# Reciprocal root in 9 instead of 12 VectorE operations; the sample tokens' convolution as one product and one sum, two heads at a time

## Chip, cores and metric

The program runs on 1 core of one Trainium2 chip. The metric is the device time of one execution in microseconds (us). Engines: TensorE (PE; its weight loads PEld overlap the matmuls), VectorE (DVE), ScalarE (ACT), GpSimd (POOL), and SyncE (SP), which issues most DMAs. Tiles live in SBUF or, behind matmuls, in PSUM banks.

## What is computed

One inference step of a two-layer trunk: 512 prompt tokens and 8 sample tokens with 1024 features. Layer 0 mixes by a gated DeltaNet (gdn), layer 1 by dilated sliding-window attention (dsw); behind each mixer stands a squared-ReLU MLP. The change touches gdn's convolution and single-token step for the sample tokens, and every 1/sqrt. The reference, cut:

```python
def l2norm(x):
    return xf * lax.rsqrt(jnp.sum(xf * xf, axis=-1, keepdims=True) + EPS)

def causal_conv_silu(x, buf, w):              # GDN_CONV = 4 taps
    xe = jnp.concatenate([buf.astype(x.dtype), x], axis=1)
    y = sum(xe[:, j:j + T] * w[j] for j in range(GDN_CONV))
    return jax.nn.silu(y), xe[:, T:]

def gdn_mixer(x, conv_buf, s0, w_in, conv_w, a_log, dt_bias, o_norm, w_out):
    ...
    qkv, new_buf = causal_conv_silu(qkv, conv_buf, conv_w)
    ...
    q = jnp.repeat(l2norm(q), rep, axis=2) * (GDN_DK ** -0.5)
    k = jnp.repeat(l2norm(k), rep, axis=2)
    beta = jax.nn.sigmoid(b.astype(f32))
    g = -jnp.exp(a_log.astype(f32)) * jax.nn.softplus(a.astype(f32) + dt_bias.astype(f32))
    o, s_new = gated_delta_chunked(q, k, v, g, beta, s0.astype(f32))
    o = rmsnorm(o, o_norm) * jax.nn.silu(z)
    y = o.reshape(B, T, GDN_V_DIM).astype(x.dtype) @ w_out
```

The recurrence is S_t = e^g S_(t-1) + beta k (v - e^g S_(t-1)^T k)^T and o_t = S_t^T q. There are 8 query/key heads, and 16 value heads of 128 x 128 states.

## The kernel before

**Stages.** Four stages follow each other on the one core: load and gdn to about 800 us, the first mlp to 1200, dsw to 1775, the second mlp to the end. The moving operand of every projection is the residual stream, features on partitions, split into a high and a low part. A projection (`proj`, L165 to L167) makes three matmuls for each of eight blocks of 128 features and each half (260 columns) of the tokens, into one of two PSUM banks called mm; then ACT or DVE empties the bank. 24 matmuls fill one bank, or 12 in the output projection of one pair, emptied by DVE in L892.

**Order.** The program text gives the dependencies. A scheduler with a simulated timeline writes the instructions of each engine in one fixed order, which the engine then works through. Six methods carry `@urgent`, a priority of 2000: decay, invert, merge, scan, sample, out. What is left fills in around them.

**gdn.** Eight pairs of value heads p = 0..7 come one after the other, each pair's first half ahead of the pair before it. For pair p:

- key: project k, sums of squares, reciprocal root "nk" (L558), and from it the columns `col` (L561 to L563).
- decay: one DMA on SP's queue reads the cumulated log-decay rows Dg into ET (L595), DVE subtracts (L596), ACT takes exponentials (L597, L598), DVE makes E (L603). ET has two buffers; one comes free after the scan of the pair before.
- invert: E's diagonal blocks go through DRAM (L629, L632), POOL solves them in 31 steps (L638, L641), and two DMAs (L642, L646) bring the result back as held<-D.
- query: project q, the sample's q and k (`sample_qk`), reciprocal root "nq" (L574).
- merge: DVE transposes (L653 to L655) behind held<-D, then PE products px (L660).
- scan: PE and DVE in turn over four chunks: pk L709, R L712, pv L715, pS L720, S L724, po L731 and L735, osb L739.
- sample: convolution of v (`sample_conv`), for each of the two heads 8 matmuls sks against its state (L816) and four DVE operations (L817 to L820), then the transpose sut of u on PE (L826), a trip through DRAM, and the state's update on POOL (L835, L838).
- out: reciprocal root "ro", DVE scales osb (L862), PE transposes otr (L867), DVE and ACT make the operand onh/onl of the output projection (L869 and the split). The last pair does it for its chunks in several cuts.

**What the change touches.** `rsqrt` (L211 to L223) makes an estimate from the bits of x in two operations (L216, L217), a factor (L218), and three rounds of three operations (L220 to L222), all on DVE. It is called 44 times: 27 times before dsw, 17 times in it. `sample_conv` (L762 to L772) is called three times for each pair: q, k, and the two v tiles together; each call makes eight DVE operations and one tanh on ACT. The history of three taps (`hist`) and the new value (`news`) lie in two parts of the stage's tile `held`.

The profile calls all small tiles base, since they are parts of one tile.

## Time and profile before

| | us |
|---|---|
| median of 3 runs | 2164.85 |
| lowest, highest run | 2163.49, 2175.41 |
| profiled execution, span from the first to the last instruction (its only time on the page) | 2168.5 |
| PE busy | 1989.6 |
| PEld busy | 1950.9 |
| DVE busy | 1349.5 |
| ACT busy | 899.4 |
| POOL busy | 535.6 |

Mean granted TensorE clock over the span: 0.950. PE is busy 92% of the span, so the time is read from where PE is not busy, and from what ended each of these idle stretches. In the rows below, a group's row has the line, engine, operation, output<-input with partitions x elements, the count, the total, the mean in ns, and the idle time before; a row of the timeline has the start and the length in us and, in brackets, the idle time before it and what ended it; a row of the waits has total, number and longest.

### The profile page before, as it was taken

Reading aid. Unit: us, or ns where it says so; the run is one execution under the profiler, and the core shown is the slowest. Engines: PE = TensorE matmul, PEld = TensorE weight load, DVE = VectorE, ACT = ScalarE, POOL = GpSimd, SP = SyncE. Lnnn points to the kernel's source line nnn. Section 1 sums busy time; section 2 is a strip of 40 time slices with the busy share of each in tenths; the row PEclk is TensorE's granted clock in tenths of the full one; section 3 lists DMA queues with packets and bytes.
Section 4 is the critical chain, followed back from the end, with each engine's and each line's share of the span. In section 5 each row is a group of like instructions: output and inputs, shape, how many; then the busy total and the mean of one; then the engine's idle time right before and its main releaser. Section 6 shows DMA issues by size and latency. Waiting matters only on the chain. (4 is left out here: it accounts for less than half of the span.)

```text
span 2168.5 us, 41683 instructions
## 1 busy us (share of the span) xinstructions
PE 1989.6 (92%) x16361; PEld 1950.9 (90%) x16361; DVE 1349.5 (62%) x3332; ACT 899.4 (41%) x2416; POOL 535.6 (25%) x821
## 2 busy tenths in 40 slices
PE   7677889896969789999999999999999989999999
PEld 6677778896969679999999999999999989999998
DVE  6754856785766584544556467676766785544544
ACT  5434444444334353223244555555555444233231
POOL 4253264355253230000002133232332250000000
PEclk8889989988979889999999999999999999999999
DMA  5334554764655538666676675534445343333332
GB/s 145 68 71 114 149 157 127 223 181 128 204 150 158 168 96 303 228 238 242 232 248 227 221 242 141 140 108 123 120 128 137 97 115 88 89 98 89 94 92 79
DMA packets 416277, 328.54 MB, mean 152 GB/s; under 512 B 48408, under 2 KB 404568, under 8 KB 413896
## 3 DMA queue, kind: packets, MB, share of 16 engines
q1 hardware_dynamic: 416080, 325.88, 50.4%
q8 instruction: 128, 2.10, 0.4%
q14 instruction: 69, 0.57, 0.1%
HBM read 302.19 MB, written 132.83 MB: 201 GB/s over the span
## 5 line engine op out<-in xcount | busy, mean ns | idle before, releaser
L165 PE MATMUL mm<-split,whi 128*128 128x260 f32 (+1 forms) x2960 | 866.7, 293 | 3.8 <-ACT split L178 2.5
L167 PE MATMUL mm<-split,wlo 128*128 128x260 f32 (+1 forms) x2960 | 851.8, 288 | 9.4 <-DVE wlo L132 9.4
L166 PE MATMUL mm<-split,whi 128*128 128x260 f32 (+1 forms) x2960 | 851.8, 288 | 8.7 <-DVE split L179 8.6
L166 PEld LDWEIGHTS mm<-split,whi 128*128 128x128 f32 (+1 forms) x2960 | 567.1, 192 | 12.3 <-DVE split L179 10.5
L167 PEld LDWEIGHTS mm<-split,wlo 128*128 128x128 f32 (+1 forms) x2960 | 566.5, 191 | 11.8 <-DVE wlo L132 10.9
L165 PEld LDWEIGHTS mm<-split,whi 128*128 128x128 f32 (+1 forms) x2960 | 567.6, 192 | 7.2 <-ACT split L178 3.7
L132 DVE TENSOR_TENSOR wlo<-raw,whi 128x1024 fp32r<-128x1024 f32 (+1 forms) x273 | 341.0, 1249 | 195.3 <-ACT whi L131 177.7
L131 ACT CAST whi<-raw 128x1024 fp32r<-128x1024 f32 (+1 forms) x273 | 285.8, 1047 | 411.7 <-PE mm L166 396.1
L167 PE MATMUL mm<-hh,wlo 128*128 128x260 f32 x1024 | 288.8, 282 | 0.0
L166 PE MATMUL mm<-hl,whi 128*128 128x260 f32 x1024 | 288.8, 282 | 0.0
L165 PE MATMUL mm<-hh,whi 128*128 128x260 f32 x1024 | 288.1, 283 | 0.0
L167 PEld LDWEIGHTS mm<-hh,wlo 128*128 128x128 f32 x1024 | 193.0, 188 | 0.0
L166 PEld LDWEIGHTS mm<-hl,whi 128*128 128x128 f32 x1024 | 192.8, 188 | 0.0
L165 PEld LDWEIGHTS mm<-hh,whi 128*128 128x128 f32 x1024 | 192.3, 188 | 0.0
L335 DVE TENSOR_TENSOR t<-mm,bc 128x260 f32<-128x260 f32 x128 | 54.8, 428 | 153.0 <-PE mm L167 153.0
L191 POOL TENSOR_TENSOR acc<-acc,sq 128x260 f32<-128x260 f32 x42 | 37.8, 909 | 382.0 <-ACT sq L190 381.3
L638 POOL TENSOR_TENSOR fs<-Ft,held 128x60 f32<-128x60 f32 (+24 forms) x248 | 100.5, 405 | 89.2 <-DMA Ft<-D 58.7
L131 ACT CAST hh<-q 128x260 fp32r<-128x260 f32 x128 | 52.5, 410 | 122.1 <-DVE q L322 122.1
L165 PE MATMUL mm<-onh,whi 128*128 128x260 f32 x256 | 90.3, 356 | 13.0 <-DVE base L892 7.9
L530 DVE SCALAR_TENSOR_TENSOR conv<-pre,held,conv 128x512 f32<-128x512 f32 x96 | 77.6, 808 | 30.1 <-POOL pre L508 27.2
L641 POOL TENSOR_TENSOR held<-held,fs 128x60 f32<-128x60 f32 (+24 forms) x248 | 90.5, 365 | 18.5
L132 DVE TENSOR_TENSOR hl<-q,hh 128x260 fp32r<-128x260 f32 x128 | 54.9, 429 | 57.0 <-ACT hh L131 57.0
(374 smaller groups left out, 3319.4 us busy)
## 6 DMA issues: line engine op xcount, KB each, us to landing
out_dram<-in_cache_kv_w_dram SPq DMA_DIRECT2D x112, 832.0 KB
raw<-in_dsw_w_in_dram SPq DMA_DIRECT2D x72, 512.0 KB
raw<-in_mlp_w_up_dram SPq DMA_DIRECT2D x64, 512.0 KB
raw<-in_mlp_w_down_dram SPq DMA_DIRECT2D x64, 512.0 KB
raw<-in_gdn_w_in_dram SPq DMA_DIRECT2D x48, 512.0 KB
S<-in_state_gdn_dram SPq DMA_DIRECT2D x16, 512.0 KB
raw<-in_gdn_w_out_dram SPq DMA_DIRECT2D x16, 512.0 KB
ub<-Du SPq DMA_DIRECT2D x16, 512.0 KB
```

What stands on the lines that cost most here:

```text
L131: nc.scalar.copy(hi, src)
L132: nc.vector.tensor_tensor(lo, src, hi.bitcast(F32), ALU.subtract)
L165: nc.tensor.matmul(ps[:m], lhsT=w[0][:, k, :m], rhs=xh[:, s], start=k == 0, stop=False)
L166: nc.tensor.matmul(ps[:m], lhsT=w[0][:, k, :m], rhs=xl[:, s], start=False, stop=False)
L167: nc.tensor.matmul(ps[:m], lhsT=w[1][:, k, :m], rhs=xh[:, s], start=False, stop=k == nk - 1)
L191: nc.gpsimd.tensor_tensor(acc[:, s], acc[:, s], t, ALU.add)
L335: nc.vector.tensor_tensor(t, ps, r2[:, s], ALU.mult)
L530: nc.vector.scalar_tensor_tensor(a, pre[:, j : j + NP], convw[:, ft, j : j + 1], a, ALU.mult, ALU.add)
L638: nc.gpsimd.tensor_tensor(tmp[:, :m, :n], Ft[:, None, j + 1 :, j].to_broadcast([P, m, n]), Uo[:, :m, j : j + 1].to_broadcast([P, m, n]), A ...
L641: nc.gpsimd.tensor_tensor(Uo[:, :m, j + 1 :], Uo[:, :m, j + 1 :], tmp[:, :m, :n], ALU.add)
```

## The change

Three edits, and all comments and docstrings go:

1. `rsqrt` makes the estimate in one operation on the bits, then one step with a polynomial in x y^2, then one Newton step: 9 operations.
2. `hist` and `news` become one part with four taps side by side. `sample_conv` takes two feature tiles at a time (q with k, and both v): one product over 128 x 64, one sum over the taps, tanh, one operation. Three calls of eight DVE operations become two of three; a pair has one tanh less.
3. `sample` makes the matmuls sks of both heads into one bank, and the four DVE operations once for both.

DVE has 308 instructions less in all: 132 in the reciprocal roots, 144 in the convolution, 32 in the sample; 257 of them stand before 800 us. ACT has 8 less; PE, POOL and SP have as many as before.

```diff
     def rsqrt(self, pool, x, eng, tag):
         n = x.shape[1]
-        y, t, z = (self.tile(pool, [P, n], F32, tag=f"{tag}{i}", name=f"{tag}{i}", bufs=2) for i in range(3))
-        yi = y.bitcast(I32)
-        self.nc.vector.tensor_scalar(yi, x.bitcast(I32), 1, None, ALU.logical_shift_right)
-        eng.tensor_scalar(yi, yi, -1.0, float(0x5F3759DF), ALU.mult, ALU.add)
-        eng.tensor_scalar(z, x, -0.5, None, ALU.mult)
-        for _ in range(3):
-            eng.tensor_tensor(t, y, y, ALU.mult)
-            eng.tensor_tensor(t, t, z, ALU.mult)
-            eng.scalar_tensor_tensor(y, t, 1.5, y, ALU.add, ALU.mult)
+        y, t, u = (self.tile(pool, [P, n], F32, tag=f"{tag}{i}", name=f"{tag}{i}", bufs=2) for i in range(3))
+        eng.tensor_scalar(y.bitcast(I32), x.bitcast(I32), -0.5, float(0x5F300000), ALU.mult, ALU.add)
+        eng.tensor_tensor(t, y, y, ALU.mult)
+        eng.tensor_tensor(t, t, x, ALU.mult)
+        eng.tensor_scalar(u, t, 0.44643426, -1.3888901, ALU.mult, ALU.add)
+        eng.tensor_tensor(u, u, t, ALU.mult)
+        eng.scalar_tensor_tensor(y, u, 1.94250179, y, ALU.add, ALU.mult)
+        eng.scalar_tensor_tensor(t, y, -0.5, y, ALU.mult, ALU.mult)
+        eng.tensor_tensor(t, t, x, ALU.mult)
+        eng.scalar_tensor_tensor(y, t, 1.5, y, ALU.add, ALU.mult)
         return y
...
-        Ufs, T64, hist, news = [part("Uf0", P), part("Uf1", P)], part("T64", 64)[:64], part("hist", 3 * NS), part("news", NS)
+        Ufs, T64, hist = [part("Uf0", P), part("Uf1", P)], part("T64", 64)[:64], part("hist", 4 * NS).rearrange("p f (b j) -> p f b j", j=CONV)
+        news = hist[:, :, :, 3]
...
-            nc.scalar.copy(hist[:, i :: 8, :], ps[:, :96].rearrange("p (s j) -> p s j", s=4))
+            nc.scalar.copy(hist[:, i::8, :, :3], ps[:, :96].rearrange("p (s b j) -> p s b j", s=4, j=3))
...
-            def sample_conv(self, i0, n, f0):
-                a, b_ = self.a, K.tile(gp, [P, 2, NS], F32, tag="sb", name="sb", bufs=12)[:, :n]
-                fs, d = slice(f0, f0 + n), slice(i0, i0 + n)
-                wj = lambda j: convw[:, fs, j : j + 1].to_broadcast([P, n, NS])
-                nc.vector.tensor_tensor(a[:, d], news[:, fs], wj(3), ALU.mult)
-                for j in range(3):
-                    nc.vector.tensor_tensor(b_, hist[:, fs, j::3], wj(j), ALU.mult)
-                    nc.vector.tensor_tensor(a[:, d], a[:, d], b_, ALU.add)
-                nc.scalar.activation(b_, a[:, d], AF.Tanh)
-                nc.vector.scalar_tensor_tensor(a[:, d], b_, 1.0, a[:, d], ALU.add, ALU.mult)
+            def sample_conv(self, i0, fs):
+                a = self.a[:, i0 : i0 + 2]
+                taps = K.tile(gp, [P, 2, NS, CONV], F32, tag="sp", name="sp", bufs=4)
+                b_ = K.tile(gp, [P, 2, NS], F32, tag="sb", name="sb", bufs=4)
+                nc.vector.tensor_tensor(taps, hist[:, fs], convw[:, fs, None, :].to_broadcast([P, 2, NS, CONV]), ALU.mult)
+                nc.vector.tensor_reduce(a, taps, axis=AX.X, op=ALU.add)
+                nc.scalar.activation(b_, a, AF.Tanh)
+                nc.vector.scalar_tensor_tensor(a, b_, 1.0, a, ALU.add, ALU.mult)
...
-                self.sample_conv(0, 1, self.fts[0])
-                self.sample_conv(1, 1, self.fts[1])
+                self.sample_conv(0, slice(self.p, self.p + 9, 8))
...
-                self.sample_conv(2, 2, self.fts[2])
+                self.sample_conv(2, slice(self.fts[2], self.fts[2] + 2))
...
+                be, eg = (sbc[:, i, 2 * p : 2 * p + 2] for i in range(2))
+                ps = K.bank("sks")
+                pst = ps[:, :32].rearrange("p (v b t) -> p v b t", v=2, t=2)
                 for v in range(2):
-                    h = 2 * p + v
-                    be, eg = sbc[:, 0, h], sbc[:, 1, h]
-                    ps = K.bank("sks")
-                    pst = ps[:, :16].rearrange("p (b t) -> p b t", t=2)
-                    S0 = self.S0s[v]
                     for b in range(NS):
-                        nc.tensor.matmul(pst[:, b], lhsT=S0[:, b], rhs=kqs[:, b], start=True, stop=True)
-                    nc.vector.tensor_tensor(u_[:, v], pst[:, :, 0], eg, ALU.mult)
-                    nc.vector.tensor_tensor(u_[:, v], a[:, 2 + v], u_[:, v], ALU.subtract)
-                    nc.vector.tensor_tensor(u_[:, v], u_[:, v], be, ALU.mult)
-                    nc.vector.tensor_tensor(o_[:, v], pst[:, :, 1], eg, ALU.mult)
+                        nc.tensor.matmul(pst[:, v, b], lhsT=self.S0s[v][:, b], rhs=kqs[:, b], start=True, stop=True)
+                nc.vector.tensor_tensor(u_, pst[:, :, :, 0], eg, ALU.mult)
+                nc.vector.tensor_tensor(u_, a[:, 2:4], u_, ALU.subtract)
+                nc.vector.tensor_tensor(u_, u_, be, ALU.mult)
+                nc.vector.tensor_tensor(o_, pst[:, :, :, 1], eg, ALU.mult)
```

With other instructions the scheduler writes another order on every engine. Three places follow, in the words of the instruction streams. Lines of the changed kernel are its own: a line L596 of before is L599 there, L520 is L523, L534 is L537, L739 is L742, L816 is L814, L817 to L820 are L815 to L818, L826 is L824, L892 is L890.

DVE in pair 2, behind the last osb of its scan (L739), before. The four operations of each head's chain are L817, L820, L818 and L819; L596 waits for the ET of the next pair:

```order
L739 TENSOR_TENSOR osb<-osb,po 128x256
L817 TENSOR_TENSOR base<-sks,held 128x8
L820 TENSOR_TENSOR base<-sks,held 128x8
L818 TENSOR_TENSOR base<-base 128x8
L819 TENSOR_TENSOR base<-base,held 128x8
L596 TENSOR_TENSOR ET<-ET,held 128x1024
L892 TENSOR_TENSOR base<-base,mm 128x260
L859 SCALAR_TENSOR_TENSOR base<-base 128x8
L892 TENSOR_TENSOR base<-base,mm 128x260
L132 TENSOR_TENSOR wlo<-raw,whi 128x1024
L817 TENSOR_TENSOR base<-sks,held 128x8
L820 TENSOR_TENSOR base<-sks,held 128x8
```

The same place on DVE in the changed kernel:

```order
L742 TENSOR_TENSOR osb<-osb,po 128x256
L599 TENSOR_TENSOR ET<-ET,held 128x1024
L857 SCALAR_TENSOR_TENSOR base<-base 128x8
L815 TENSOR_TENSOR base<-sks,held 128x16
L818 TENSOR_TENSOR base<-sks,held 128x16
L816 TENSOR_TENSOR base<-base 128x16
L817 TENSOR_TENSOR base<-base,held 128x16
L890 TENSOR_TENSOR base<-base,mm 128x260
L820 TENSOR_TENSOR base<-base 128x16
```

One chain for both heads now stands behind ET's subtraction, where one head's chain stood ahead of it and the other's behind it. The joint chain stands behind L599 in pairs 1, 2, 3 and 5 too, ahead of it in pairs 0 and 4, and in pair 6 behind the transposes of merge.

PE in pair 2 from the end of the scan to sut, the changed kernel (S_2541 and S_2543 are the two heads' states, mm<-onh or onl the output projection, mm<-split the next projection; the run of twelve mm is three rows four times over, shown once):

```order
L738 MATMUL po<-S,kq 128x256
L814 MATMUL sks<-base,S_2541 128x2 x8
L814 MATMUL sks<-base,S_2543 128x2 x8
L165 MATMUL mm<-onh,whi 128x260
L166 MATMUL mm<-onl,whi 128x260
L167 MATMUL mm<-onh,wlo 128x260
...
L824 MATMUL sut<-base 16x128
L165 MATMUL mm<-split,whi 128x260
```

Before, the same twelve mm stood between the two heads' sks, and 35 mm of the next projection between the second sks and sut: 47 matmuls beside the sks, where 12 stand now. In the other pairs it is 57 before and 20 now (pair 0), 44 and 22, 24 and 12 (pair 3), 30 and 28, 44 and 30, 24 and 12 (pair 6).

DVE at the first two waits for ET, about 77 to 93 us of the profile, before (L520 scales the first projections, L521 the sample's part of them, and L534 makes the first value tile's input, conv, complete somewhat later):

```order
L222 SCALAR_TENSOR_TENSOR base<-base 128x4
L596 TENSOR_TENSOR ET<-ET,held 128x1024
L534 SCALAR_TENSOR_TENSOR conv<-tanh,conv 128x512
L561 TENSOR_TENSOR base<-held,base 128x8
L596 TENSOR_TENSOR ET<-ET,held 128x1024
L520 TENSOR_TENSOR pre<-pre,bc 128x512
L521 TENSOR_TENSOR held<-held,bc 128x8
```

The same place in the changed kernel:

```order
L537 SCALAR_TENSOR_TENSOR conv<-tanh,conv 128x512
L523 TENSOR_TENSOR pre<-pre,bc 128x512
L576 TENSOR_SCALAR base<-base 128x20
L524 TENSOR_TENSOR held<-held,bc 128x8
L599 TENSOR_TENSOR ET<-ET,held 128x1024
L851 TENSOR_SCALAR base<-base 128x4
L216 TENSOR_SCALAR base<-base 128x16
L770 TENSOR_TENSOR base<-held 128x64
L533 SCALAR_TENSOR_TENSOR conv<-pre,held,conv 128x512
L599 TENSOR_TENSOR ET<-ET,held 128x1024
```

L520's successor now stands ahead of both waits for ET instead of behind them.

More of the change, by code (lines that the diff above doesn't have):

```diff
@@ L374, in gdn @@
         gp = setup.enter_context(tc.tile_pool(name="gset", bufs=1))
-        sizes = dict(Uf0=U * P, Uf1=U * P, T64=U * 64, hist=32 * 3 * NS, news=32 * NS, eyeU=8 * 32, convw=32 * CONV, tri=P, Uo0=8 * 32, Uo1=8 * 32, tail=32 * 3, beg=160, gcl=128, egc=192, sbc=256, id8=8, onorm=1, alog=16, dtb=16, bat=160)
+        sizes = dict(Uf0=U * P, Uf1=U * P, T64=U * 64, hist=32 * 4 * NS, eyeU=8 * 32, convw=32 * CONV, tri=P, Uo0=8 * 32, Uo1=8 * 32, tail=32 * 3, beg=160, gcl=128, egc=192, sbc=256, id8=8, onorm=1, alog=16, dtb=16, bat=160)
         held = cp.tile([P, sum(sizes.values())], F32, name="held")
```

## The prediction

> **What bounds the kernel now.** I read first the span, then the engines' busy times by stage (windows of the trace), then the waits of TensorE and VectorE in the one stage where TensorE waits.
>
> ```profile
> span 2168.5 us, 41683 instructions
> ...
> core 0: us, PE busy (x) PEld busy (x) DVE busy (x) ACT busy (x) POOL busy (x), PEclk, DMA share, GB/s
> 0.00:800.00 800.00, 649.12 (x5217) 620.88 (x5218) 540.22 (x1536) 333.50 (x966) 325.21 (x657) 0.87 0.52 145
> ...
> 1200.00:1775.00 575.00, 553.92 (x4599) 545.86 (x4598) 401.10 (x1057) 296.21 (x945) 177.03 (x120) 1.00 0.51 144
> ```
>
> The windows shown are load with gdn, and dsw; the two mlp stages, left out, hold no edit. TensorE (PE) is idle for 800 - 649.1 = 150.9 us in the first and 575 - 553.9 = 21 us in the second, so what an edit on VectorE (DVE) can win lies nearly all in the first 800 us. There the granted clock (PEclk) averages 0.87, in dsw 1.00: 0.13 x 800 = 104 us of full-speed time are lost beside the idle time.
>
> ```profile
> PE sut L826 <- DVE base L819: 34.5, 5, 13.2
> PE px L660 <- DMA held<-D: 21.4, 3, 11.3
> PE pk L709 <- DVE S L724: 8.7, 5, 4.2
> PE mm L166 <- DVE split L179: 8.1, 4, 5.4
> PE mm L165 <- DVE base L892: 7.9, 3, 6.4
> PE sut L826 <- DVE base L767: 2.7, 1, 2.7
> DVE ET L596 <- DMA ET<-Dg: 40.3, 8, 8.2
> DVE held L653 <- DMA held<-D: 37.7, 5, 9.9
> ```
>
> These are waits in 0 to 800 us: total, times, longest. PE's largest are for DVE, at the lines that the change touches (sut, the transpose of the sample's u). But DVE itself sits idle 40.3 + 37.7 = 78 us on DMAs, in L596 (E and ET of the next pair) and L653 (merge). An engine that works its list in order and stands before a DMA is not made faster by fewer instructions ahead of that place.
>
> **What leaves DVE.**
>
> ```profile
> L221 DVE TENSOR_TENSOR base<-base 128x24 f32<-128x24 f32 (+7 forms) x132 | 28.8, 219 | 2.3
> L222 DVE SCALAR_TENSOR_TENSOR base<-base 128x24 f32<-128x24 f32 (+7 forms) x132 | 27.1, 206 | 2.7
> L220 DVE TENSOR_TENSOR base<-base 128x24 f32<-128x24 f32 (+7 forms) x132 | 24.9, 190 | 2.4
> L770 DVE TENSOR_TENSOR base<-base 128x8 f32<-128x8 f32 (+1 forms) x72 | 18.0, 251 | 0.3
> L769 DVE TENSOR_TENSOR base<-held 128x8 f32<-128x8 f32 (+1 forms) x72 | 14.9, 216 | 3.5 <-ACT held L419 3.1
> L767 DVE TENSOR_TENSOR base<-held 128x8 f32<-128x8 f32 (+1 forms) x24 | 6.8, 285 | 0.0
> L772 DVE SCALAR_TENSOR_TENSOR base<-base 128x8 f32<-128x8 f32 (+1 forms) x24 | 4.5, 187 | 0.5 <-ACT base L771 0.5
> L474 DVE TENSOR_TENSOR held<-held 128x64 f32<-128x64 f32 x1 | 0.2, 224 | 0.0
> L1255 DVE TENSOR_REDUCE base<-mxt 1x8 f32<-1x128 f32 x8 | 2.2, 272 | 0.0
> ```
>
> Each line: total us, then mean ns of one. Reciprocal root: 396 of its instructions take 80.8 us, 204 ns each; 44 calls go from 12 to 9, so 132 x 0.204 = 26.9 us less. Convolution: 192 instructions of 44.2 us become 48. The two new forms don't occur in the trace. The product over 128x64 is bounded by L474, 0.224, and the slower L767, 0.285; the sum over taps by nothing below L772's 0.187 and L1255's 0.272, which runs through 128 elements of a partition where the new one runs through 64. I take 0.224 (the same size) and 0.272: 16 x (0.224 + 0.272 + 0.187) = 10.9, so 33.3 less; the other ends move it by 1.4 us. The sample's u: 64 instructions become 32, about 6 less at L772's price. Together 66 us by full durations. But independent small instructions follow each other faster than they last:
>
> ```profile
> 251.11 0.16 DVE L772 SCALAR_TENSOR_TENSOR base<-base 128x8 f32<-128x8 f32 x1
> 251.19 0.16 DVE L216 TENSOR_SCALAR base<-base 128x4 int32<-128x4 int32 x1
> ...
> 255.41 0.30 DVE L222 SCALAR_TENSOR_TENSOR base<-base 128x4 f32<-128x4 f32 x2
> ```
>
> L772 lasts 0.16 us, and L216 starts 0.08 after it. At that price the 308 instructions that go are worth 25 us. So DVE has 25 to 66 us less to do, 257/308 of it before 800 us: 21 to 55 of 540, 4 to 10%. What of this reaches the end is counted place by place.
>
> **Term A, the first values' transposes.**
>
> ```profile
> 83.00 0.69 DVE L520 TENSOR_TENSOR pre<-pre,bc 128x512 f32<-128x512 f32 x1
> ...
> 93.06 0.69 DVE L534 SCALAR_TENSOR_TENSOR conv<-tanh,conv 128x512 f32<-128x512 f32 x1
> 93.90 1.09 PE L694 MATMUL vtr<-base,conv 128*128 128x128 f32 x4 [11.76 <-DVE base L221]
> ```
>
> The transposes read conv, so what released them is L534's end at 93.75, not the L221 that the row names. DVE needs 10.06 us from L520 to that L534, for 35 instructions. In the new order L520's successor stands ahead of both waits for ET, some 20 instructions stand between the second wait and this end, and PE has 38 instead of 20 matmuls between the two groups of transposes. About 15 instructions less at that pace, with L520's 0.69 among them, is 2.7 us; 18 matmuls at a spacing of 0.12 (below) are 2.2 us of cover. I take **-5**; ends: 0, if the wait for ET moves as much later, and -11.8, the whole wait.
>
> **Term B, the tail.**
>
> ```profile
> 778.87 1.60 DVE L221 TENSOR_TENSOR base<-base 128x4 f32<-128x4 f32 x1
> 780.53 2.34 POOL L838 TENSOR_TENSOR S<-S,ub 128x1024 f32<-128x1024 f32 x1
> 780.60 2.29 DVE L222 SCALAR_TENSOR_TENSOR base<-base 128x4 f32<-128x4 f32 x1
> 783.81 1.11 PE L867 MATMUL otr<-base,osb 128*128 128x128 f32 x4 [7.48 <-DVE osb L862]
> ```
>
> In the last pair PE waits 7.48 us on a reciprocal root whose L222 takes 2.29 us beside POOL's L838, though it has 128x4 elements and 0.21 as its mean; the L221 before it takes 1.60 instead of 0.22. With three instructions fewer ahead, the last may be done before L838 starts. I take **-3**, L222's 2.1 and most of three instructions at 0.37 (term D); ends: 0 (the stall falls on L862 instead) and -4.6, L221's 1.4 as well.
>
> By the Trainium skill, GPSIMD Engine Reference, section "Specifications", GpSimd's SBUF interface is shared with VectorE, with contention for VectorE instructions that have two SBUF inputs. L222 reads two tiles, so the trace agrees; but L862, the next that PE waits for, does too, and by this rule the stall would merely go over to it, for -0.7 instead of -3.
>
> **Term C, the sample's chain.** The rows are those of pair 2.
>
> ```profile
> 355.43 0.37 SPq L595 DMA_DIRECT2D ET<-Dg  x1
> 364.04 1.37 DVE L596 TENSOR_TENSOR ET<-ET,held 128x1024 f32<-128x1024 f32 x1 [5.79 <-DMA ET<-Dg]
> 364.62 0.28 PE L165 MATMUL mm<-split,whi 128*128 128x260 f32 x1
> 364.74 0.28 PE L166 MATMUL mm<-split,whi 128*128 128x260 f32 x1
> 367.90 0.38 PE L826 MATMUL sut<-base 128*16 128x128 f32 x1 [2.88 <-DVE base L819]
> 368.51 0.42 PE L166 MATMUL mm<-split,whi 128*128 128x260 f32 x1
> 368.73 0.42 PE L167 MATMUL mm<-split,wlo 128*128 128x260 f32 x1
> ```
>
> The first head's chain ran ahead of L596, the second's behind it and behind L132. In the new order there is one chain for both, directly behind the wait for ET. It ends some 1.4 us sooner, as L132 (1.21) now follows it, but sut stands behind 12 matmuls of projections instead of 47: 35 x 0.12 = 4.2 us that covered the wait now come after it. Net +2.7; I take +2.5 here and in pair 1, which the order changes alike (44 to 22). In pair 4 the chain now stands ahead of the wait for ET, so sut needn't wait; but the projections behind it need DVE to empty their two banks, so I give it -2. In pair 0, whose sut wait is the 2.7 row, the chain is ahead too: -2.7. Pairs 3, 5 and 6 have no clear sign. Sum **0**; ends: -11.3 (pair 4's whole wait, the second longest) and +15 (2.5 in each of six pairs).
>
> **Term D, merge.** px waits for DMAs that end a chain which begins with the key's reciprocal root: 12 instructions from 251.19 to 255.41, 4.4 us, 0.37 each among others. Three fewer are 1.1 us, in three waits **-3**; ends: 0 and twice that.
>
> **Term E, the other DVE waits** (pk 8.7, L166 8.1, L165 7.9; 24.7 together) shrink with DVE's work by 4 to 10%, or more where a wait is the end of a long list: **-2**; ends 0 and -5.
>
> **Term F, the clock.** 104 us lost beside 151 idle is 0.69 us for each idle us. The rows of C show it: matmuls 0.12 apart before the wait of 2.88, 0.22 after. A shorter gap does not always spare its slow stretch, so for 13 us of shorter gaps I take a third of 9: **-4** with rounding up, ends 0 and -9.
>
> **Term G, dsw.** 17 of the 44 roots stand behind 1200 us, where PE is busy 554 of 575: **-1**. The 8 ACT instructions fewer are nothing, ACT being busy 333 of 800 us.
>
> Sum: -5 - 3 + 0 - 3 - 2 - 4 - 1 = -18. The profiled execution is known only by its span, 2168.5; that is 3.65 over the median of the runs, 2164.85. 2168.5 - 18 = 2150.5, and against the median **2147**.
>
> **The rivals.**
>
> No change, about 2161: what DVE saves it waits away at L596 and L653. For it: the 78 us, and that DMA issue to L596's start is 8.6 us in pair 2, which nothing here shortens. Against it: A and B have no DMA between the saving and PE's wait. Only B and G remain, -4. Chance 0.27.
>
> Slower, about 2181: a longer list stands behind each wait for ET. The joint chain costs PE its cover in six pairs, +15 of waits, and as each is followed by matmuls at half pace, +10 for the clock (15 x 0.69); A, which hangs on two such waits, is at its end of 0. The other gains are B, D, E and G, -9: +16. It decides once sut's waits sum to more than 37.2 + 9 / 1.69 = 42.5 us. For it: pairs 1 and 2 in the order. Against it: pairs 0 and 4. Chance 0.18.
>
> Much faster, about 2123: long gaps go and their slow clock with them. 25 us of idle time less, as the low ends of A and B, half of C's and D, at 1.69 each: -42. For it: 0.87 in one stage alone, behind its gaps. Against it: most long gaps end on a DMA. Chance 0.13. The Trainium skill, TensorE: Matmul & The Clock Gate, section "HAM oscillation", has the rule "no PE-idle gaps >~3.4µs": by it only gaps brought below that size win clock, here A's and the tail's at most. The trace disagrees in part, since the gap of 2.88 us is followed by the slow spacing.
>
> **How the numbers follow.** The forecast has 0.42. A measurement of this kernel tells about 0.5% from no change, 10.8 us, so faster is under 2154.0 and slower over 2175.7. The forecast and the much faster case give 0.49 to faster, leaving 0.06 of the forecast's spread to "same" with the 0.27: 0.33; slower 0.18. Low end: the much faster case with half of px's 21.4 gone too, 2112. High end: the slower case with its clock price half as large again, 5 us, 2186. Beyond both I leave about 0.15. The forecast's own range is 2130 to 2160.
>
> **What would show it.** A: the wait of vtr at about 94 us falls to about 7. B: no reciprocal-root instruction above 1 us near the tail, and otr's wait near 4.5. C: sut's waits stay at 37 +- 5; above 42.5 the slower rival holds. D: px waits of about 18. F: PEclk 0.88 or more in the first stage. DVE's busy time must fall by 25 to 66; if it does while L596 and L653 wait 20 us more, "no change" was right. Wrong altogether would be a difference outside the first 800 us, or a new long wait of PE there.

## The result and the profile after

| kernel | median us | range (runs) | ratio to before, 95% interval | span of the profiled execution, mean clock |
|---|---|---|---|---|
| before | 2165.52 | 2163.49 to 2175.41 (5) | | 2168.5, 0.950 |
| changed | 2183.27 | 2182.61 to 2192.68 (5) | 1.0081 [1.0059, 1.0103] | 2181.5, 0.943 |

The change makes the kernel 0.8% slower, 17.75 us, where the forecast was about 18 us faster. First the head of the page and two stages of the windows (duration, busy us with instructions of PE, PEld, DVE, ACT and POOL, then PEclk, DMA share, GB/s) of the changed kernel.

```profile
span 2181.5 us, 41479 instructions
PE 2001.5 (92%) x16361; PEld 1966.1 (90%) x16361; DVE 1309.0 (60%) x3024; ACT 899.5 (41%) x2408; POOL 527.3 (24%) x821
...
0.00:800.00 800.00, 647.96 (x5174) 622.72 (x5175) 500.08 (x1265) 327.84 (x944) 309.39 (x651) 0.85 0.51 142
1200.00:1775.00 575.00, 559.88 (x4617) 553.03 (x4617) 388.12 (x1014) 297.01 (x962) 175.84 (x118) 0.99 0.52 148
```

DVE has 40.5 us less to do (1349.5 before), inside the 25 to 66 forecast, and 40 of it in the first stage (540.2 to 500.1). TensorE gained nothing from that. Two sums that are used for every run below show why. **Idle** is the span less PE's busy time: 2168.5 - 1989.6 = 178.9 before, 2181.5 - 2001.5 = 180.0 after. **Slow clock** is the span times (1 - mean clock): 108.4 before, 124.3 after. So of the 13 us between the two spans idle time has +1, slow clock +16, and what is left of the span -4. The split is rough, since the mean clock counts idle time too. Two further figures bear it out. By the clock records of the two traces, half of the time in which PE is busy at 0.50 is 77.0 us before and 91.9 after. And the mean of slow clock over all executions with a clock on record, not the profiled one alone, is about 104 us for the kernel before and 124.5 for the changed one. So the loss is on the side of the clock.

Waits of PE in 0 to 815 us, and those of DVE for ET and held<-D, changed kernel (total, times, longest):

```profile
PE sut L824 <- DVE base L817: 39.0, 6, 12.4
PE px L663 <- DMA held<-D: 22.3, 4, 9.9
PE pv L718 <- DVE R L715: 12.7, 5, 6.8
PE vtr L697 <- DVE conv L537: 11.1, 1, 11.1
PE kqt L584 <- DVE ot L867: 9.2, 2, 5.6
PE kqt L584 <- DVE kq L537: 7.4, 2, 4.4
PE mm L167 <- DVE wlo L132: 6.5, 1, 6.5
PE mm L165 <- ACT held L518: 6.5, 1, 6.5
PE pk L712 <- DVE S L727: 6.3, 2, 3.3
PE mm L166 <- DVE split L179: 6.1, 3, 5.1
PE otr L865 <- DVE osb L860: 2.2, 2, 1.2
DVE ET L599 <- DMA ET<-Dg: 50.9, 7, 16.4
DVE held L656 <- DMA held<-D: 49.0, 6, 12.0
DVE held L657 <- DMA held<-D: 3.8, 2, 3.6
```

DVE now waits 99.9 us at L599 and L656, where it waited 78.0 at the same two lines. But in the kernel before a further wait for held<-D stands at the next transpose, which the prediction's 78 us leave out:

```profile
DVE held L654 <- DMA held<-D: 13.6, 2, 13.4
```

With these rows (and 0.2 us at L658 of the changed kernel) DVE waits 103.9 us for the two DMAs, where it waited 91.6. So 12 of the 40 us that it saves are waited away before DMAs. On PE some waits are gone (otr's 7.48, the 7.9 on L892), and others of the same size are new (kqt, L167, L165).

Where the 12.7 us between the last instructions of the two timelines arise is read from the starts of the same instructions:

| instruction | before | changed | difference |
|---|---|---|---|
| sut of pair 6 | 718.37 | 717.35 | -1.0 |
| first pk of the last pair | 746.1 | 751.2 | +5.1 |
| last mm of gdn's output projection | 801.9 | 807.7 | +5.8 |
| first mm of mlp0's down projection | 849.7 | 862.9 | +13.2 |
| first matmul of dsw | 1177.0 | 1191.0 | +14.0 |
| last instruction | 2163.2 | 2175.9 | +12.7 |

**The first place, 717 to 751 us, is the merge of the last pair**, whose px and pu stand on PE between projections. Timeline and windows of the kernel before:

```profile
718.37 0.37 PE L826 MATMUL sut<-base 128*16 128x128 f32 x1 [13.16 <-DVE base L819]
722.76 0.69 PE L660 MATMUL px<-held,E 32*32 32x32 f32 x16
...
718.00:722.30 4.30, 3.93 (x19) 3.96 (x20) 3.19 (x11) 0.26 (x1) 0.00 (x0) 0.50 0.03 6
722.30:731.00 8.70, 8.70 (x133) 7.97 (x133) 6.75 (x18) 3.04 (x7) 3.40 (x2) 0.99 0.65 220
```

And of the changed kernel:

```profile
717.35 0.37 PE L824 MATMUL sut<-base 128*16 128x128 f32 x1 [10.96 <-DVE base L817]
720.67 1.06 PE L663 MATMUL px<-held,E 32*32 32x32 f32 x16
...
717.00:720.60 3.60, 3.25 (x15) 3.12 (x15) 2.46 (x9) 0.88 (x2) 0.00 (x0) 0.50 0.01 2
720.60:740.50 19.90, 19.90 (x158) 18.12 (x157) 13.49 (x26) 4.67 (x10) 8.57 (x4) 0.50 0.45 146
740.50:751.00 10.50, 9.80 (x83) 9.59 (x82) 9.35 (x21) 2.86 (x6) 0.00 (x0) 1.00 0.84 250
```

In both kernels PE comes out of a wait of over 10 us at half clock. Before, the clock is back at 722.3, just before px begins (its 16 records take 0.69 us). In the changed kernel px comes first (1.06 us for its 16), and the clock stays at 0.50 for 19.90 us more although PE is busy for every one of them. The wait for sut is the shorter one here, 10.96 against 13.16.

**The second place is the start of mlp0.** PE is idle 5 of the 25 us behind 800 in the changed kernel, and none before, as the windows of the kernel before and of the changed kernel show:

```profile
800.00:825.00 25.00, 25.00 (x208) 24.57 (x207) 16.53 (x31) 13.89 (x31) 5.78 (x7) 1.00 0.42 122
```
```profile
800.00:825.00 25.00, 20.08 (x144) 19.16 (x143) 16.43 (x34) 14.54 (x33) 9.96 (x12) 0.88 0.45 132
...
818.56 1.04 ACT L131 CAST whi<-raw 128x1024 fp32r<-128x1024 f32 x1 [1.90 <-DMA raw<-in_mlp_w_up_dram]
819.65 0.58 PE L165 MATMUL mm<-split,whi 128*128 128x260 f32 x1 [3.54 <-ACT whi L131]
```

PE waits for ACT, which waits for a load of the up projection's weights. Of these loads, SP's queue (timeline) of the kernel before issues three ahead of the 64 small writes of the convolution buffers that begin at 779.86:

```profile
749.86 1.47 SPq L146 DMA_DIRECT2D raw<-in_mlp_w_up_dram  x1
...
765.79 0.38 SPq L146 DMA_DIRECT2D raw<-in_mlp_w_up_dram  x1
...
777.59 0.48 SPq L146 DMA_DIRECT2D raw<-in_mlp_w_up_dram  x1
...
811.65 2.41 SPq L146 DMA_DIRECT2D raw<-in_mlp_w_up_dram  x3
```

The changed kernel's issues one ahead of these writes, which begin at 786.43 there, with loads of gdn's output weights in the other two places, and the next ones only at 814:

```profile
750.11 0.37 SPq L146 DMA_DIRECT2D raw<-in_gdn_w_out_dram  x1
...
756.95 0.37 SPq L146 DMA_DIRECT2D raw<-in_gdn_w_out_dram  x1
...
768.58 0.38 SPq L146 DMA_DIRECT2D raw<-in_mlp_w_up_dram  x1
...
814.40 2.03 SPq L146 DMA_DIRECT2D raw<-in_mlp_w_up_dram  x3
```

SP's list was not edited: it was redrawn with everything else. No run was made on this second place alone, but the traces of the kernels below tell what it goes with. In the 60 us behind the last mm of gdn's output projection, PE is idle for 4.6 to 5.5 us in the four kernels that have the changed kernel's TensorE order, and not at all in the other fifteen. So this place belongs to the drawn order.

### The profile page after: what moved, and what is told of

Its sections match the earlier page's. It is cut to its first block, busy times and chain, and to the rows that moved or that the text cites. A ratio compares the mean times of both kernels' runs of the same rounds, so it can differ in the third digit from the quotient of the medians.

```text
span 2181.5 us, 41479 instructions
## 1 busy us (share of the span) xinstructions
PE 2001.5 (92%) x16361; PEld 1966.1 (90%) x16361; DVE 1309.0 (60%) x3024; ACT 899.5 (41%) x2408; POOL 527.3 (24%) x821
## 4 chain that ended last, share of the span: by engine, by line
PE 64%; DVE 12%; DMA 9%; POOL 7%; issue 3%; ACT 3%; SPq 0%; DVEq 0%; POOLq 0%; ACTq 0%
PE mm L165 18%; PE mm L167 18%; PE mm L166 18%; POOL fs L641 3%; POOL held L644 3%; DMA ET<-Dg 2%; DVE wlo L132 2%; DMA Ft<-D 2%; DMA D<-held 2%; PE po L1201 1%; ACT P L1129 1%; DVE base L1241 1%; PE tr L1054 1%; DMA X<-base 1%; DVE conv L533 1%
## 5 line engine op out<-in xcount | busy, mean ns | idle before, releaser
L165 PE MATMUL mm<-split,whi 128*128 128x260 f32 (+1 forms) x2960 | 871.8, 295 | 17.0 <-ACT held L518 6.5
L167 PE MATMUL mm<-split,wlo 128*128 128x260 f32 (+1 forms) x2960 | 859.9, 291 | 8.1 <-DVE wlo L132 8.1
L166 PE MATMUL mm<-split,whi 128*128 128x260 f32 (+1 forms) x2960 | 856.9, 290 | 6.6 <-DVE split L179 6.6
L165 PEld LDWEIGHTS mm<-split,whi 128*128 128x128 f32 (+1 forms) x2960 | 574.0, 194 | 20.8 <-ACT held L518 6.9
L167 PEld LDWEIGHTS mm<-split,wlo 128*128 128x128 f32 (+1 forms) x2960 | 572.2, 193 | 10.7 <-DVE wlo L132 9.6
L166 PEld LDWEIGHTS mm<-split,whi 128*128 128x128 f32 (+1 forms) x2960 | 573.2, 194 | 9.3 <-DVE split L179 7.8
L167 PE MATMUL mm<-hh,wlo 128*128 128x260 f32 x1024 | 289.4, 283 | 0.0
L166 PE MATMUL mm<-hl,whi 128*128 128x260 f32 x1024 | 288.7, 282 | 0.0
L165 PE MATMUL mm<-hh,whi 128*128 128x260 f32 x1024 | 288.5, 283 | 0.0
L166 PEld LDWEIGHTS mm<-hl,whi 128*128 128x128 f32 x1024 | 192.9, 188 | 0.0
L167 PEld LDWEIGHTS mm<-hh,wlo 128*128 128x128 f32 x1024 | 192.8, 188 | 0.0
L165 PEld LDWEIGHTS mm<-hh,whi 128*128 128x128 f32 x1024 | 192.3, 188 | 0.0
L165 PE MATMUL mm<-onh,whi 128*128 128x260 f32 x256 | 89.6, 351 | 0.2 <-ACT onh L131 0.2
```

Source lines behind the costliest of these rows:

```text
L165: nc.tensor.matmul(ps[:m], lhsT=w[0][:, k, :m], rhs=xh[:, s], start=k == 0, stop=False)
L166: nc.tensor.matmul(ps[:m], lhsT=w[0][:, k, :m], rhs=xl[:, s], start=False, stop=False)
L167: nc.tensor.matmul(ps[:m], lhsT=w[1][:, k, :m], rhs=xh[:, s], start=False, stop=k == nk - 1)
```

## The experiments

**The theories.** (1) The order: what the edits take out is worth about what was forecast, and the scheduler's new order of the first stage costs more. (2) The work: the new instructions themselves, or DVE's DMA waits, eat the gain, whatever the order. (3) A single place, the last pair's merge at half clock, is the loss.

**Work and order apart.** At the end of the kernel a table adds edges between neighbours on an engine. They order issue alone, and no wait on another engine is added:

```diff
+def in_order(tc, nc):
...
+    for e, text in ORDER.items():
...
+        for a, b in zip(at, at[1:]):
+            tc.add_manual_dep(
+                by[e][b], by[e][a].name, mybir.DependencyInfo(mybir.DependencyClass.NoSync, mybir.DependencyReason.DATA), reason="order"
+            )
...
         tile_step(tc, I, O)
+        in_order(tc, nc)
```

"Old ops" is the kernel before and "new ops" the changed one; the table holds TensorE's list of one or the other up to the end of gdn. Two of the four are controls, in which a kernel is tied to its own list.

> A control: the kernel before, with TensorE's instructions of the first two stages (4300 or so, up to the end of gdn) tied to the order that they had anyway; the other engines are ordered freely around it. Both theories: as before, 2160 to 2172 us. If it lies outside, tying an order changes something itself, and the three runs beside it must be read against this one.

> The changed kernel's instructions, with TensorE's tied to the order of the kernel before. Theory O (the order): the loss sits in the new order, so it is gone here: 2148 to 2166, with the slow-clock stretch of 31 us near 710 us back to 17 or less and three loads of mlp weights before the end of gdn instead of one. Theory W (the work): the new instructions cost by themselves (the product takes 444 ns, the joint chain for two heads stands behind ET): 2176 to 2190.

> The instructions of the kernel before, with TensorE's tied to the order of the changed kernel. Theory O: the order alone makes it slow: 2178 to 2200, more than the changed kernel if its 308 VectorE instructions fewer help there. Theory W: 2160 to 2170, as before.

> The second control: the changed kernel with TensorE's instructions tied to its own order. Both theories: as the changed kernel, 2178 to 2190.

| | before's TensorE order | changed kernel's TensorE order |
|---|---|---|
| old ops | 2181.42 (2177.66 to 2183.14, 4 runs), idle 190.1, slow clock 115.5 | 2221.16 (2218.93 to 2227.1, 4), 205.0, 164.7 |
| new ops | 2149.51 (2145.53 to 2150.64, 4), 172.4, 92.4 | 2176.94 (2166.84 to 2182.98, 10), 177.3, 106.1 |

The kernel before took 2166.99 beside them. The expectation for the new ops in before's order was met in all its parts: the time, a slow stretch of 13.6 us at sut of pair 6 (30.7 in the changed kernel), and three loads of mlp weights ahead of the writes. Two were missed upwards: the first control by 9 us and the old ops in the new order by 21. The second control came out 1 us below its range, and 6 below the changed kernel. Read down, the edits save 32 us in the one order and 44 in the other. Read across, the new order costs 27 us with the new ops and 40 with the old. The control on the old order is itself 14 us off; VectorE's list was still free around TensorE's, which the next control bears on. So the signs are plain (the ranges in each row and column are apart), and the sizes are good to perhaps 15 us. Idle time and slow clock are those of the profiled execution, and for the new ops in the new order that is the fastest of ten (span 2165.1, clock 0.951). Over all executions, slow clock is 114.4 and 148.2 us with the old ops, 93.9 and 125.0 with the new ones. So the 27 us that the new order costs the new ops go with 31 us of slow clock.

Starts of the same instructions show where it arises. Against the new ops in before's order, the changed kernel is 16.2 us later at sut of pair 6 (717.3 for 701.1), 24.0 at the last mm of the output projection (807.7 for 783.7) and 31.5 at the first mm of mlp0's down projection (862.9 for 831.4). So about a quarter arises at the start of mlp0, the second place above, and the rest is spread over gdn.

The new ops in the old order are also **the fastest version of all by median**, 2149.51 or 0.9901 [0.9882, 0.9920] of before: faster than both kernels.

**The same with three engines tied, and the merge moved.** In the first two, the instructions that both kernels have on TensorE, ScalarE and VectorE stand in before's order, and what was added or removed on VectorE is free between them. SyncE's and GpSimd's lists stay free. The third has the changed kernel's TensorE list with one edit, in the last pair: 24 projection matmuls go ahead of the merge's px and pu.

```diff
 L167 MATMUL mm<-onh,wlo 128x260
+L165 MATMUL mm<-onh,whi 128x260
+L166 MATMUL mm<-onl,whi 128x260
+L167 MATMUL mm<-onh,wlo 128x260
...
 L663 MATMUL px<-held,E 32x32 x8
...
 L685 MATMUL pu_7859<-X_7848,held 64x64 x8
-L165 MATMUL mm<-onh,whi 128x260
-L166 MATMUL mm<-onl,whi 128x260
-L167 MATMUL mm<-onh,wlo 128x260
...
```

> The control again, tied more closely: the kernel before with the instructions of TensorE, ScalarE and VectorE that both kernels have in common tied to the order of before, up to the end of gdn. If the 14 us that the first control lost came from VectorE's order around TensorE's, it is at 2160 to 2172 now. If tying costs something by itself, it stays at 2176 or more.

> The changed kernel's instructions on the same three orders of before. Theory O: the work that goes is worth 10 to 30 us once the order stays: 2138 to 2157. Rival: only TensorE's order mattered, and the first run of this kind was lucky around it: 2158 to 2170.

> The changed kernel with TensorE's own order, but for one place: in the last pair the small matmuls of merge (32x32 and 64x64 px and pu) stand 24 projection matmuls later, still ahead of the scan. Theory C (clock): after the long gap before sut only full-size matmuls bring the clock back, so the slow stretch of 34 us that begins near 693 shrinks to 17 to 24, and the time falls by 4 to 9 us from the 2177 of the run without the edit. Rival: the clock comes back by time or by TensorE being busy, whatever it runs: the stretch stays at 31 or more, and the time within 2 us.

The control is near before now, at the upper end of its range: 2172.59 (2170.63 to 2177.5) against 2168.93. The new ops take 2156.64 (2151.18 to 2161.36), 0.9949 [0.9935, 0.9964]: the work saves 16 us, and theory 2 falls. The merge moved later gave 2174.22 (2168.52 to 2180.17), which can't be told from the 2176.94 of the same order without the move, where 4 to 9 us less were expected. Its windows at the place, without the move and then with it:

```profile
708.00:710.50 2.50, 2.50 (x12) 2.50 (x13) 1.41 (x8) 0.88 (x2) 0.00 (x0) 0.50 0.02 3
710.50:727.50 17.00, 17.00 (x144) 15.18 (x142) 11.26 (x26) 4.19 (x9) 5.98 (x3) 0.50 0.54 171
727.50:737.00 9.50, 8.03 (x67) 7.54 (x67) 9.48 (x17) 2.02 (x5) 3.65 (x2) 0.99 0.76 233
```
```profile
716.60:720.00 3.40, 3.40 (x17) 3.40 (x17) 2.35 (x8) 0.88 (x2) 0.00 (x0) 0.51 0.01 2
720.00:737.00 17.00, 16.93 (x188) 15.56 (x188) 16.77 (x40) 6.24 (x14) 5.55 (x2) 0.90 0.68 213
```

The mechanism works at this place: with full-size matmuls first, 0.90 is granted through the 17 us of the merge instead of 0.50. But the end hardly moves, so theory 3 explains the place and not the loss. Theory 1 is left: no single place accounts for its 27 us.

**The clock by itself.** Behind the kernel's work, four stretches of matmuls whose results nobody uses, each behind a pause that VectorE makes. The third comes out of its pause straight into a mixture, 16 of 32x32 to 2 of 128x260; the fourth has 60 full ones ahead of the same mixture. The small ones have plain f32 operands and the full ones fp32r, as in the kernel's merge and projections, so size and type are not told apart.

```diff
+    def mixed(ps, n):
+        for _ in range(n):
+            small(ps, 16)
+            full(ps, 2)
...
+    pause(ps, 8)
+    full(ps, 8)
+    mixed(ps, 24)
+    full(ps, 60)
+    pause(ps, 8)
+    full(ps, 60)
+    mixed(ps, 24)
+    full(ps, 60)
```

> The kernel before with four stretches of unused matmuls behind it: 100 full ones (128x128 by 260 columns); the same after a pause of about 10 us; after a second pause 8 full ones, then 24 times (16 small ones of 32x32 and 2 full ones), then 60 full ones; after a third pause 60 full ones, then the same mixture, then 60 full ones. Theory C: the second stretch is back at full clock 4 to 9 us after its pause; the third stays at half clock through its whole mixture, some 30 us; in the fourth the clock is back before the mixture and stays at 1.0 through it. Rival: in the third the clock is back after 4 to 9 us as in the second. The time is longer than before by about 100 us and says nothing else.

Windows of the second, third and fourth stretch (the matmuls of the second start at 2179.9):

```profile
2170.00:2184.70 14.70, 4.80 (x22) 4.81 (x23) 9.08 (x8) 0.41 (x1) 0.00 (x0) 0.54 0.00 0
2184.70:2192.00 7.30, 7.30 (x63) 7.30 (x63) 0.00 (x0) 0.00 (x0) 0.00 (x0) 1.00 0.01 2
...
2205.50:2273.40 67.90, 67.90 (x844) 60.82 (x845) 0.00 (x0) 0.00 (x0) 0.00 (x0) 0.50 0.01 1
...
2294.00:2304.20 10.20, 10.20 (x162) 9.52 (x161) 0.00 (x0) 0.00 (x0) 0.00 (x0) 1.00 0.01 2
2304.20:2362.20 58.00, 58.00 (x725) 52.03 (x723) 0.00 (x0) 0.00 (x0) 0.00 (x0) 0.50 0.01 2
```

Full-size matmuls bring the clock back 4.8 us after the pause. In the third stretch it stays at 0.50 for 67.9 us, through 8 full matmuls, the 61 us of the mixture and 4.9 us of full ones behind it. In the fourth it is back at 1.00 before the mixture begins at 2298.9, and the mixture pulls it down 5.3 us later without any pause, with PE busy all the time. That half of theory C failed: 1.0 was expected through the mixture. So idle time is not the only thing that lowers the clock; what PE is busy with counts too. What this is worth in the kernel is not shown: the one merge that was moved changed the end by less than the runs scatter.

**The parts on the fixed order.** One or two parts of the change alone, all on before's order of three engines. "Root" is the 9-operation reciprocal root, "conv" the convolution with four taps together, "joint" one chain for both heads in the sample's u; "two chains" is root and conv without joint:

```diff
-                be, eg = (sbc[:, i, 2 * p : 2 * p + 2] for i in range(2))
...
+                for v in range(2):
+                    h = 2 * p + v
+                    be, eg = sbc[:, 0, h], sbc[:, 1, h]
...
-                nc.vector.tensor_tensor(u_, a[:, 2:4], u_, ALU.subtract)
+                    nc.vector.tensor_tensor(u_[:, v], a[:, 2 + v], u_[:, v], ALU.subtract)
...
```

> The kernel before with the reciprocal root in 9 operations alone, on the three orders of before (control: 2172.6, all three edits: 2156.6). If a saving goes by the number of VectorE instructions, 132 of 308: 2163 to 2168. If it goes by chains on the path (the terms B and D and most of A in the prediction are roots): 2156 to 2162. Rival: a single edit saves nothing, as DMAs take it all, 2170 to 2174.

> The kernel before with the convolution as a product and a sum alone, on the three orders of before. By number of instructions, 144 of 308: 2162 to 2168. If only chains on the path count: 2168 to 2173, as no term of the prediction but a part of A hangs on it.

> The kernel before with the joint chain for both heads alone (32 VectorE instructions fewer), on the three orders of before; control 2172.6, all three edits 2156.6, root alone 2173.5, convolution alone 2176.1. If the joint chain is what gains on that order (one chain for two while TensorE keeps its 35 matmuls of cover): 2154 to 2164. If the gain needs all three edits together, or the single runs are each off by chance: 2168 to 2176.

> Root and convolution together, two chains as before, on the three orders of before. If the joint chain is what gains: 2170 to 2178, as either of the two alone. If the number of instructions counts: 2156 to 2164.

| on before's order | median us (range) | against the control's 2172.6 |
|---|---|---|
| root | 2173.47 (2168.86 to 2175.39) | +0.9 |
| conv | 2176.05 (2170.88 to 2180.01) | +3.5 |
| joint | 2169.95 (2167.07 to 2179.29) | -2.6 |
| root and conv (two chains) | 2158.52 (2153.43 to 2167.13) | -14.1 |
| all three | 2156.64 (2151.18 to 2161.36) | -16.0 |

The rows come from three jobs, beside which the kernel before took 2168.93 (control and all three), 2167.43 (root, conv) and 2169.35 (joint, two chains); so a difference under about 2 us says nothing. By the expectations, root lies in its rival's range, conv 3 us above all of its ranges, joint in the range for no gain, and two chains in that for the number of instructions. Neither root nor conv saves anything alone, and together they save 14 us. Most of that is clock again: over all executions, slow clock is 108.8 us in the control, 111.8 with root, 110.7 with conv and 97.8 with both. Why they have to come together stays open; SyncE's and GpSimd's lists were free in all five, so a redraw of these is not ruled out. The joint chain costs nothing where the order is kept: -2.6 alone, -1.9 on top of the other two.

**The parts with the scheduler free**, and the scheduler stirred by a small edit elsewhere, two warm-up matmuls fewer:

```diff
-WARM = 24
+WARM = 22
```

> The same 9-operation root alone, with the order left to the scheduler. Theory O: what the new order does has nothing to do with which instructions went, so it can come out anywhere from 2150 to 2190, and differs from the run on the old order by 5 us or more. Rival: the loss belongs to another part of the change (the joint chain or the convolution), and the root alone gives 2155 to 2165 with either order.

> The changed kernel with the sample's two heads one after the other again, each with its own bank and chain as before; order left to the scheduler. If the joint chain is what makes it slow (the slower rival of the prediction): 2145 to 2162. Theory O: no better than the changed kernel for that reason; anywhere from 2150 to 2190, and its idle time about the same, with the difference in the time lost to the slow clock.

> The kernel before with the root in 9 operations and the joint chain, convolution as before, order left to the scheduler. Without the joint chain the same gave 2152.6. Theory J (a joint chain leads the scheduler to poor orders): 2172 to 2200, like the two free orders with it (2183.3, 2197.9). Theory O (any draw): nothing ties it to those; 2150 to 2172 is as likely as more.

> The kernel before with the same edit. Theory O: it moves by 5 us or more either way, 2150 to 2185. Rival: 2162 to 2170.

> The changed kernel with 22 instead of 24 warm-up matmuls at its very start, order left to the scheduler: an edit of half a microsecond while the inputs come in, which gives another order of TensorE in gdn. Theory O (the loss is the draw of an order): it moves by 5 us or more from 2183.3, most likely to 2150 to 2175, since this order was the worst of those drawn freely. Rival: the loss is bound to the change's own instructions: 2178 to 2188.

> Root and convolution with two chains as before, order left to the scheduler, and 22 warm-up matmuls for another draw. With 24 it was 2164.4. Theory J: again under 2170. Theory O: it can be anywhere from 2150 to 2200, over 2172 in one of two cases.

| free order | median us (range) | ratio to before, 95% interval | idle, slow clock |
|---|---|---|---|
| root | 2152.57 (2146.45 to 2157.22) | 0.9931 [0.9904, 0.9959] | 176.0, 96.9 |
| two chains | 2164.44 (2155.82 to 2174.33) | 0.9985 [0.9966, 1.0003] | 172.0, 97.1 |
| before, 22 warm | 2162.43 (2160.35 to 2168.7) | 0.9971 [0.9957, 0.9986] | 177.5, 97.3 |
| two chains, 22 warm | 2168.10 (2163.37 to 2169.96) | 0.9996 [0.9972, 1.0019] | 178.6, 104.0 |
| root and joint | 2186.28 (2177.14 to 2191.9) | 1.0081 [1.0054, 1.0109] | 182.2, 128.8 |
| changed, 22 warm | 2197.89 (2185.83 to 2200.31) | 1.0115 [1.0077, 1.0154] | 187.8, 142.9 |

The kernel before took 2167.4 to 2169.4 in these jobs. Two things follow. An edit that has nothing to do with gdn moves a kernel by -7 to +15 us through the order alone, which is nearly as much as the whole effect forecast. And whatever has the joint chain and a free order is slow: 2183, 2186 and 2198, against 2153 to 2169 for the five without it. Since the chain costs nothing in the old order, it is the orders that it leads the scheduler to. The last two runs were made to test this (theory J), and both came out as it says, 2186.28 and 2168.10; theory O had the changed kernel with 22 warm-up matmuls at 2150 to 2175 most likely, and it took 2197.89.

What these orders have in common can be counted: between the scan's last po and sut, over pairs 0 to 6, TensorE has 264 to 277 projection matmuls in the traces of the five without the chain, and 130 to 144 in those of the three with it. That is what the order listing had shown (pair 4 of the kernel before has 36 in its trace, where 30 was given). Yet the waits for sut don't follow the time. Root and joint, one of the slow three, has the least of the eight (0 to 830 us):

```profile
PE sut L826 <- DVE base L819: 17.5, 5, 5.5
```

They are 40.0 us in the slowest, 34.2 in the fastest and 37.2 before. The loss is slow clock, 124 to 143 us against 97 to 108, and it is there by the end of gdn: the last mm of the output projection starts at 807.7 to 834.4 in the three, at 788.9 to 802.6 in the five. That the missing cover brings the slow clock about is argued from this, not shown: one merge was moved, and the end didn't follow.

## Why the forecast was wrong

**The step that failed** is the one that priced the change as edits to a list that otherwise stays: the sum of places A to G, with term C at 0 ("no clear sign" for three pairs), and no term for the rest of the order. The redrawn order, for which the sum had nothing, is +27 with the new ops and goes with 31 us of slow clock. The work's share is near in size, -18 forecast against -16 measured with three engines tied and -32 with TensorE tied, but this doesn't bear out the terms. B, D and most of A hang on roots, and root alone on the fixed order, which should then have come to 2156 to 2162, took 2173.47. So that the sizes agree is luck in part.

The prediction's sign of being wrong altogether, a difference outside the first 800 us, came true too: 7.4 of the 12.7 us arise between 808 and 863, at the start of mlp0, which no term looked at.

**A, the first transposes** (-5, wait near 7): half right. The wait stayed at 11.1 for 11.8, but PE reached it earlier, so it ended 4 us sooner, at 89.9 for 93.9. Of that, 3.1 were left at the first px, after two new gaps at kqt of 3.0 and 4.4 us.

**B, the tail** (-3): the wait of 7.48 is gone, but not for the reason given. A root's instruction still stands beside POOL's L836 and takes 2.02 us, which fails the promised mark of 1 us (timeline, changed kernel):

```profile
781.61 2.38 POOL L836 TENSOR_TENSOR S<-S,ub 128x1024 f32<-128x1024 f32 x1
781.99 2.02 DVE L223 TENSOR_TENSOR base<-base 128x4 f32<-128x4 f32 x1
...
782.35 0.36 PE L165 MATMUL mm<-onh,whi 128*128 128x260 f32 x1
784.99 0.44 PE L865 MATMUL otr<-base,osb 128*128 128x128 f32 x2 [0.97 <-DVE osb L860]
```

This agrees with the shared-port rule quoted there (the Trainium skill, GPSIMD Engine Reference, section "Specifications"), since L223 reads two tiles; but the stall stayed with the root and did not go over to the scaling (L860, 0.69 us). The wait is only 0.97 because the new order has output projections left for PE there, and the stage's last mm is 5.8 us later all the same.

**C, the sample's chain** (0): sut's waits are 39.0 for 37.2, inside 37 +- 5. The slower rival put its turning point at 42.5 and so was not met by its own mark, though it named the right part of the change. Its price ran through waits. What the chain cost came through the order and the clock. That this rival's time, 2181, is so near the measured 2183.27 is luck: it put +15 on the waits for sut, where +1.8 was measured, and +10 on the clock through these waits.

**D, merge** (-3): failed, px waits 22.3 for 21.4, where 18 was forecast. **E** (-2): the waits named there fell (pk 8.7 to 6.3, L166 8.1 to 6.1, L165 on L892 gone), and new ones came, kqt 16.6 together. A list of waits shrinks line by line and keeps its sum: 178.9 to 180.0.

**F, the clock** (-4, PEclk 0.88 or more): wrong in sign, 0.85 for 0.87. The term tied the clock to the length of gaps at 0.69 us for each idle us. Idle time stayed, and slow clock rose by 16 us. Its 104 us of lost time also held idle time itself: by the clock records 77.0 us fall on time in which PE was busy. The probe shows what the term lacked: small matmuls hold or pull the clock down with no gap at all. The rule on gaps that was weighed there (the Trainium skill, TensorE: Matmul & The Clock Gate, section "HAM oscillation") speaks of idle time alone, and could not give this either.

**G, dsw** (-1): about right. Idle time in the window of dsw fell from 21 to 15 us, but from dsw's first matmul to the last instruction the changed kernel gains only 1.3 us (+14.0 to +12.7).

The two unknown prices, in the changed kernel's groups (total us, mean ns):

```profile
L770 DVE TENSOR_TENSOR base<-held 128x64 f32<-128x64 f32 x16 | 7.1, 444 | 0.0
L771 DVE TENSOR_REDUCE base<-base 128x16 f32<-128x64 f32 x16 | 3.4, 210 | 0.0
L773 DVE SCALAR_TENSOR_TENSOR base<-base 128x16 f32<-128x16 f32 x16 | 3.0, 188 | 0.3 <-ACT base L772 0.3
```

And the product by its line (ns of the shortest, median and longest):

```profile
L770 DVE TENSOR_TENSOR base<-held x16: 211/218/1928, 60.2 to 720.9; 128x64 f32<-128x64 f32 x16
```

They sum to 13.5 us where 10.9 was taken. The product's price was right, 0.218 as a rule for the 0.224 taken. Its mean is 0.444 because two of the sixteen last 1.93 us; both (at 545.4 and 642.7) stand beside an L833 of GpSimd of 2.3 us and end with it. The sum over taps was below what was taken (0.210 for 0.272). At 2.6 us this decided nothing. The "no change" rival's mechanism, waiting away before DMAs, was real: its own mark, 20 us more at L596 and L653, was met with 21.9, of which 12.3 are left when the next transposes are counted. But the time rose, so its mark didn't tell it from what happened.

## What to carry to other kernels

Where a scheduler draws the order, price an edit twice: what it takes out, and what a redraw is worth. Stir the order by an edit that should do nothing (here two warm-up matmuls: -7 to +15 us) before reading a difference of that size as the edit's own, and try the edited kernel on the old order, which here turned +0.8% into -1.0% with TensorE tied and -0.5% with three engines tied. Split a difference in span into idle time and slow clock before looking for a wait: here no list of waits holds the loss.

## What the runs showed of the chip

Matmuls of 32x32 (plain f32) mixed with a few full ones (fp32r) kept TensorE at a granted clock of 0.50 for as long as they lasted (61 us of the 67.9), and took it from 1.00 to 0.50 without a pause, 5.3 us after they began (58.0 us at 0.50), at 100% busy. Full-size matmuls restored it 4.8 us after a pause. It is in the kernel too: the merge's px and pu behind a wait held 0.50 for 19.9 us, and the same kind of work behind a few us of full matmuls, with more full ones between, ran at 0.99.

A VectorE product of two SBUF operands that takes 0.218 us as a rule took 1.93 us beside a GpSimd operation of 2.32 us (L833) that had started 0.47 us earlier; the two ended within 0.1 us of each other. L223, in the rows above, likewise ended with POOL's L836, at 784.0.
